# One more pair of up-projection strips by half-size products, and a new order of the steps around it

## The chip, the cores and the metric

The kernel runs on one core of one Trainium2 chip. The metric is device time of that core in microseconds (us): the median of three runs of the kernel before is 671.82 us (671.79 to 672.07). Times in traces count from the start of the profiled span. The engines are TensorE (PE; PEld is its weight load), VectorE (DVE), ScalarE (ACT), GpSimd (POOL) and SyncE (SP, which here only issues transfers).

## The reference, cut to what matters

One decoder layer: a mixing sub-layer, then a gated MLP with a causal convolution of width 3 between the up-projection and the activation. The change lies in the second sub-layer (512 tokens, model width 1024, hidden width 2816, all f32):

```python
h2 = rmsnorm(x, norm2_g[l]) * (1.0 + sc2) + sh2
u = causal_dwconv(h2 @ w_up[l], conv_w[l], conv_b[l])      # w_up: 1024 x 5632
a, v = jnp.split(u, 2, axis=-1)
x = x + gt2 * ((jax.nn.silu(a) * v) @ w_down[l])
```

## The kernel before, in words

**Strips.** The 5632 columns of `w_up` are 44 strips of 128. Strip st = 2f + s belongs to hidden block f (0 to 21); s = 0 is its half of `a`, s = 1 its half of `v`. Each strip ends up in one PSUM bank of 128 x 512 (`us[st]`). The normed input is kept as tiles `h2h` and `h2l`.

**High and low parts.** Every f32 operand is split into a high part, which ScalarE casts to the matmul's type, and a low part, the rest. A product is then three matmuls (`mm3`, lines 156 to 158): high by high, high by low, low by high; the last of the three is the first to read the weights' low part. `split` (lines 152 and 153) makes the low part by a VectorE subtraction. The adding form makes it without VectorE: ScalarE writes the negated rounded weights (line 263 or 1707), GpSimd issues a transfer that adds the weights to them in place (line 264 or 1708), and ScalarE casts the high part (line 265 or 1709).

**Two ways to multiply a strip pair.** A plain strip is 24 matmuls of 512 columns. The two strips of an even block f = 2j can instead be done together by seven half-size products (the Winograd scheme on 2 x 2 blocks: two strips, two halves of the 1024 inner rows, two halves of the 512 tokens). Each of the seven, P1 to P7, is 12 matmuls of 256 columns. It needs sums of the four weight quarters (`ns`, `nc`, `na`, `s4`: VectorE, in place on the loaded weights or in tile `e`), seven split forms of 512 columns (`n1` and `n5`, both in the single buffer of tile `w`, and `f2`, `f3`, `f4`, `f6`, `f7` in tiles `wq`), and four split sums of the input halves (`hS`, made once by the steps `t`). P1 adds up in `us[4j+1]`; `S` (ScalarE) copies that first result to the other strip's bank before P6 goes on in the same bank; P5 goes to a bank of its own, `ux`; `w` (ScalarE) copies that to SBUF; `V` and `W` (VectorE) add it back.

**Order.** Nothing reorders: each engine's queue runs in the order in which two strings of tokens are walked. `PRO` is the opening sequence (strips 0 to 7), `UNIT` is walked once for each j from 2 to 10 (strips 4j to 4j+3: a pair by half-size products, then two plain strips, cut into B0, B1 and C0, C1). A token with a prime prepares unit j + 1. M3 to M7 multiply plain strips, F and A split their weights (A by the adding form), q0 to q7 and p take a finished strip through the convolution (`up_post`, lines 1639 to 1655: an activation on ScalarE, a pair of VectorE steps, for s = 0 a silu on ScalarE, for s = 1 the gating product), x runs one piece of later work (sums and splits for the down-projection: `gP`, `gQ`, `st`, `s`), g and G advance the adaLN gate, m0 and m1 split the plain strips of a unit, h0 and h1 cast their high parts where these come later. In units j > 2 both low parts come by the adding form, in unit 2 only the second (line 1729).

**Loads.** SyncE loads the weights of one block (two strips) into one of three `raw` buffers (line 223); a load waits until the buffer's last readers are done.

Of the kernel before, what the change touches and what calls it, by code (L numbers as in the profile page):

```python
# [24 lines left out]
KT = D // P  # L25
# [15 lines left out]
NB = 2  # L41
NU = 10
AWAY = (0, 1, 2, 3, 4, 5)
CUT = {"B": 6, "C": 7}
ADD = (1, 1)
PLAIN = ""
PRO = ("t t x M1 M2 t t t t F3 M3 F4 t A5 q0 G M4 q1 q2 F6 q3 M5 G M6 A7 x q4 x q5 G x t x n1' ns' f2' nc' n5' q6 na' s4' m0' x x M7 m1' g x f6' f7' x x x x f4'")
UNIT = ("P1 S P5 w n1' ns' x f3 B0 P6 P2 B1 V x f2' nc' n5' h1 x p-1 f4' P7 x m0' P3 h0' W K p2 g na' p0 C0 P4 x x x C1 s4' p1 x m1' x f6' x x x f7'")
PREP = ('sq2 sq3 rq2 rq3', '', 'nq0', 'fq0', 'nq1', '', 'lq0', 'fq1', 'nq2', '', 'lq1', 'fq2', 'nq3', 'lq2', 'fq3',
        'lq3', 'sk0 rk0 sk1 rk1', 'nk0 fk0 sk2 rk2', 'nk1 fk1 sk3 rk3', 'lk0 nk2 fk2', 'lk1 nk3 fk3 sa0 ra0',  # L50
# [61 lines left out]
def hybrid_layer_kernel(ctx: ExitStack, tc: tile.TileContext, d: dict, out: bass.AP, dbg=None):  # L112
# [1552 lines left out]

    def h2_form(o, q):
        hS[q] = hi, lo = [G([4, 256], F32R, s="hS") for _ in range(2)]
        split(hi, lo, hB.pop(o))

    tw = [(h2_sum, (0, 0), (0, 1), (0, 0)), (h2_sum, (0, 1), (1, 1), (0, 1)), (h2_sum, (1, 1), (1, 1), (0, 0)),  # L1670
          (h2_form, (0, 0), 1), (h2_sum, (1, 0), (1, 0), (1, 1)), (h2_form, (1, 1), 2), (h2_form, (0, 1), 3),
# [7 lines left out]
    def half_form(src):  # L1679
        t = G([2, 4, P], F32R, s="wq")  # L1680
        split(t[:, 0], t[:, 1], src)
        return t[:, 0], t[:, 1]

    def pair_open(j):
        raw = take(f"up{2 * j}")
        quads[j] = [raw[:, s, 4 * h:4 * h + 4] for s in range(2) for h in range(2)]
        t = wp.tile([P, 2, KT, P], F32R, tag="aw", name=nm("w3"), bufs=1)
        forms7[j] = {n: (t[:, 0, h:h + 4], t[:, 1, h:h + 4]) for n, h in ((1, 0), (5, 4))}
        split(*forms7[j][1], quads[j][0])
# [35 lines left out]
    def std_make(j, s):  # L1725
        st = 4 * j + 2 + s
        if s == 0:
            raws[j] = take(f"up{2 * j + 1}")
        wts[st], high[st] = std_form(raws[j][:, s], ADD[s] and (s or j > NB))

    def seed(o, src):
        sc.copy(o, src)
# [3 lines left out]
        sc.copy(ws5[j], us["x", j][:, lo_half])  # L1736

    def banks(j):
        us[4 * j + 1] = PS("u")
        us["x", j] = PS("ux")  # L1740
        us[4 * j] = (held.pop if j == NU else held.get)(0)

    ws5 = {}

    def u_of(j, n, sl):
        return us[4 * j + n][:, sl]

    def do(j, tok):
        last = j == NU
# [8 lines left out]
    def do_(j, tok):  # L1758
        last = j == NU
        lo_, hi_ = lo_half, hi_half  # L1760
        w = forms7.get(j)
        u = partial(u_of, j)
        if tok == "P1":
            banks(j)
            sprod(u(1, lo_), w[1], h2_quarter(0, lo_), True)
            if last:
                pe.matmul(u(1, hi_), w[1][0][:, 0], h2_quarter(0, lo_)[0][0], start=False, stop=False,
                          skip_group_check=True)
        elif tok == "P5":
            sprod(us["x", j][:, lo_], w[5], h2_summed(1), True)  # L1770
        elif tok == "P6":
            sprod(u(1, lo_), w[6], h2_summed(2))
        elif tok == "P2":
            sprod(u(0, lo_), w[2], h2_quarter(1, lo_))
        elif tok == "P7":
            sprod(u(1, lo_), w[7], h2_summed(3))
        elif tok == "P3":
            sprod(u(0, hi_), w[3], h2_quarter(1, hi_))
        elif tok == "P4":
            sprod(u(1, lo_), w[4], h2_summed(4))  # L1780
        elif tok in ("B0", "B1", "C0", "C1"):
            up_mm(4 * j + (2 if tok[0] == "B" else 3), full, (range(0, CUT[tok[0]]), range(CUT[tok[0]], KT))[int(tok[1])])
        elif tok == "S":
            sc.copy(u(0, lo_), u(1, lo_))
        elif tok == "w":
            spare(j)
        elif tok == "V":
            ve.tensor_tensor(u(0, hi_), u(1, lo_), ws5[j], ALU.add)
        elif tok == "W":
            ve.tensor_tensor(u(1, hi_), u(1, lo_), ws5[j], ALU.add)  # L1790
        elif tok[0] == "p":
            up_post(4 * j + int(tok[1:]))
        elif tok == "x":
            step(1)
        elif tok in ("g", "G"):
            gate_step(2 if tok == "g" else 1)
        elif tok == "t":
            turn()
        elif tok[0] == "m":
            std_make(j, int(tok[1]))  # L1800
        elif tok[0] == "h":
            h = high.pop(4 * j + 2 + int(tok[1]))
            if h:
                h()
        elif tok == "K":
            park_late()
        elif tok == "n1":
            pair_open(j)
        elif tok == "ns":
            pair_sum(j)  # L1810
        elif tok == "nc":
            pair_less(j, 2, 0, 2)
        elif tok == "na":
            pair_less(j, 0, 4, 0)
        elif tok == "s4":
            pair_less(j, 1, 1, 0)
        elif tok == "n5":
            split(*w[5], quads[j][4])
        else:
            pair_form(j, int(tok[1]), {6: 0, 2: 1, 7: 2, 3: 1, 4: 3}[int(tok[1])])  # L1820
# [183 lines left out]
    for tok in PRO.split():  # L2004
        if tok[0] == "M":
            up_mm(int(tok[1]), full if tok[1] > "2" else hi_half)
            if tok == "M2":
                held[0] = us[0]
        elif tok[0] in "FA":
            piece(added=tok[0] == "A")  # L2010
            wts[int(tok[1])] = ahead.pop(0)
        elif tok[0] == "q":
            up_post(int(tok[1]))
        elif tok[0] in "txgG":
            do_(1, tok)
        else:
            do(NB - 1, tok)
# [111 lines left out]
```

## Time and profile before

| | us |
|---|---|
| median of three runs | 671.82 |
| profiled execution, its own time | 672.72 |
| its span | 670.9 |
| TensorE busy in the span | 663.2 |
| VectorE busy | 582.8 |
| ScalarE busy | 400.5 |
| last plain matmul run of the opening sequence starts (M7) | 367.0 |
| unit 2 starts (its P1) | 372.44 |
| unit 3 starts | 393.47 |
| down-projection starts | 562.25 |

A row of the timeline gives start, length, engine, line, operation, and written tile <- read tiles with their shapes; in brackets the idle time of that engine before it and what ended it. Consecutive rows of one engine overlap a little, so an engine's pace is read from starts.

### The profile page before, as it was taken

The page shows a single profiled execution, that of the slowest core. Times are in us where ns is not written, and L with a number is a line of the kernel's source. Part 1 is how long each engine was busy: PE and PEld are TensorE (multiplying, and loading weights), DVE is VectorE, ACT ScalarE, POOL GpSimd, SP SyncE. Part 2 cuts the span into 40 slices and gives each one's busy share as a digit, 9 for nine tenths or more (in the row PEclk, how much of TensorE's full clock was granted, in tenths as well). Part 3 has the DMA queues.
Part 4 walks back from the last instruction along what each step waited for, and adds up shares of the span by engine and source line. Part 5 has one row for each costly group of instructions (what it writes and reads, how often), then busy time and mean ns, then how long its engine had stood idle before and what let it go on. Part 6 is the DMA issues. An engine that isn't in the chain of part 4 may idle for free.

```text
span 670.9 us, 11080 instructions
## 1 busy us (share of the span) xinstructions
PE 663.2 (99%) x4072; PEld 567.9 (85%) x4072; DVE 582.8 (87%) x1173; ACT 400.5 (60%) x775; POOL 74.1 (11%) x100
## 2 busy tenths in 40 slices
PE   8999999999999999999999999999999999999997
PEld 4677898788898889888998989999899998888886
DVE  4688988999998997789988999888988888988787
ACT  5565446766677688334665776577765775553431
POOL 1006144200100000211100111010110110000000
PEclk9999999999999999999999999999999999999999
DMA  9999443398042132537436488877889759999932
GB/s 278 286 321 271 149 157 130 100 293 264 26 149 95 33 103 96 195 103 220 153 95 157 103 228 240 239 214 211 228 236 250 224 153 345 366 343 398 380 111 95
DMA packets 111880, 134.84 MB, mean 201 GB/s; under 512 B 7322, under 2 KB 84946, under 8 KB 111826
## 3 DMA queue, kind: packets, MB, share of 16 engines
q1 hardware_dynamic: 102961, 106.89, 50.2%
q0 software_dynamic: 4720, 16.26, 10.7%
q10 hardware_dynamic: 4144, 10.99, 4.3%
q8 instruction: 32, 0.52, 0.3%
q14 instruction: 23, 0.18, 0.1%
HBM read 107.11 MB, written 16.00 MB: 183 GB/s over the span
## 4 chain that ended last, share of the span: by engine, by line
PE 91%; SPq 3%; DMA 2%; DVE 2%; issue 1%; ACT 0%; ACTq 0%; DVEq 0%
PE u L157 11%; PE u L156 11%; PE u L158 11%; PE dn L157 5%; PE dn L156 5%; PE dn L158 5%; PE pT L156 3%; PE pT L158 3%; PE pT L157 3%; PE F L1063 3%; PE oT L1091 3%; PE oh L158 2%; PE oh L156 2%; PE oh L157 2%; PE lev L1192 2%; SPq L321 2%
## 5 line engine op out<-in xcount | busy, mean ns | idle before, releaser
L156 PE MATMUL u<-h2h,whi 128*128 128x512 f32 (+1 forms) x200 | 75.1, 375 | 0.0
L157 PE MATMUL u<-h2l,whi 128*128 128x512 f32 (+1 forms) x200 | 74.9, 374 | 0.0
L158 PE MATMUL u<-h2h,wlo 128*128 128x512 f32 (+1 forms) x200 | 74.5, 373 | 0.0
L158 PEld LDWEIGHTS u<-h2h,wlo 128*128 128x128 f32 x200 | 37.7, 189 | 6.8
L1031 ACT ACTIVATE pt<-pt,mx 128x128 f32<-128x128 f32 (+3 forms) x64 | 35.8, 562 | 12.1 <-DVE mx L1015 11.1
L156 PEld LDWEIGHTS u<-h2h,whi 128*128 128x128 f32 x200 | 37.9, 189 | 5.5
L157 PEld LDWEIGHTS u<-h2l,whi 128*128 128x128 f32 x200 | 37.9, 189 | 5.2
L156 PE MATMUL pT<-hT,whi 128*128 128x512 f32 x96 | 39.2, 409 | 0.0
L153 DVE TENSOR_TENSOR wlo<-raw,whi 128x1024 fp32r<-128x1024 f32 (+1 forms) x31 | 36.0, 1161 | 3.6 <-ACT whi L152 3.4
L1651 ACT ACTIVATE y<-y 128x512 f32<-128x512 f32 x22 | 13.9, 633 | 41.7 <-DVE y L1648 41.6
L158 PE MATMUL pT<-hT,wlo 128*128 128x512 f32 x96 | 37.7, 393 | 0.0
L157 PE MATMUL pT<-hT,whi 128*128 128x512 f32 x96 | 37.6, 392 | 0.0
L152 ACT CAST whi<-raw 128x1024 fp32r<-128x1024 f32 (+1 forms) x31 | 30.9, 998 | 10.4 <-PE kva L158 4.4
L1647 DVE SCALAR_TENSOR_TENSOR y<-u,cv,y 128x511 f32<-128x511 f32 x44 | 32.8, 745 | 5.0 <-ACT y L1646 5.0
L1070 ACT COPY pT<-F 128x512 f32<-128x512 f32 (+2 forms) x52 | 25.8, 502 | 15.4 <-PE F L1063 11.2
L1015 DVE CUSTOM_DVE_ANT_0 pt<-S,cmask 128x128 f32<-128x128 f32 (+3 forms) x64 | 29.7, 485 | 5.7 <-PE S L1010 5.6
L1648 DVE SCALAR_TENSOR_TENSOR y<-u,cv,y 128x510 f32<-128x510 f32 x44 | 32.9, 749 | 1.5
L397 POOL TENSOR_TENSOR hrs<-hrs,mhalf 128x4 f32<-128x4 f32 (+2 forms) x16 | 20.9, 1314 | 120.7 <-DVE hrs L396 120.6
L1646 ACT ACTIVATE y<-u,cv 128x512 f32<-128x512 f32 x44 | 33.8, 770 | 0.0
L1708 POOL DMA_DIRECT2D wlo<-raw x17 | 14.6, 859 | 166.2 <-ACT wlo L1707 74.6
L153 DVE TENSOR_TENSOR wq<-raw,wq 128x512 fp32r<-128x512 f32 x45 | 30.7, 685 | 0.5 <-ACT wq L152 0.5
L158 PE MATMUL u<-hS,wq 128*128 128x256 f32 x108 | 30.6, 284 | 0.0
(471 smaller groups left out, 2175.3 us busy)
## 6 DMA issues: line engine op xcount, KB each, us to landing
raw<-in_w_up SPq DMA_DIRECT2D x44, 512.0 KB, 5.7
aw<-in_w_ada SPq DMA_DIRECT2D x24, 512.0 KB, 3.8
raw<-in_w_down SPq DMA_DIRECT2D x10, 1024.0 KB, 5.4
wlo<-raw POOLq DMA_DIRECT2D x19, 512.0 KB, 5.2
ada<-in_w_ada SPq DMA_DIRECT2D x32, 256.0 KB, 5.9
raw<-in_w_in SPq DMA_DIRECT2D x7, 1024.0 KB, 6.0
rawd<-in_w_down SPq DMA_DIRECT2D x12, 512.0 KB, 10.5
pk<-st ACTq DMA_DIRECT2D x11, 512.0 KB, 6.5
```

Of the source, the lines that this page charges most:

```text
L152: sc.copy(hi, src)
L153: (eng or ve).tensor_tensor(lo, src, f32(hi), ALU.subtract)
L156: pe.matmul(o, ah, bh, start=start, stop=False, skip_group_check=True)
L157: pe.matmul(o, ah, bl, start=False, stop=False, skip_group_check=True)
L158: pe.matmul(o, al, bh, start=False, stop=stop, skip_group_check=True)
L397: gp.tensor_tensor(o, o, mhalf[:, 0:n], ALU.pow)
L1015: ve.tensor_tensor_reduce(pt[:, sl], ps[:, sl], cmask[:, 512 - W:512], -1.0, 1e30, ALU.add, ALU.min, mx[:, e:e + 1])
L1031: sc.activation(pt[:, sl], pt[:, sl], AF.Exp, bias=mx[:, e:e + 1], scale=-1.0, accum_out=su[:, h % 2, e:e + 1])
L1070: sc.copy(pT, ps[:, 0:n * P])
L1646: sc.activation(y, u, AF.Identity, bias=cv[:, 132 + c:133 + c], scale=cv[:, 88 + c:89 + c])
L1647: ve.scalar_tensor_tensor(y[:, 1:], u[:, :T - 1], cv[:, 44 + c:45 + c], y[:, 1:], ALU.mult, ALU.add)
L1648: ve.scalar_tensor_tensor(y[:, 2:], u[:, :T - 2], cv[:, c:c + 1], y[:, 2:], ALU.mult, ALU.add)
```

## The change

Block 3 (strips 6 and 7), which the opening sequence multiplied as two plain strips, becomes a tenth pair by half-size products, as "unit 1" with strips `base(1)` = 6 and 7. Its weights are taken as soon as token `no` is met. Strip 5 (M5) is multiplied in two pieces, Y0 and Y1, between those products. The opening string is written anew, with the preparation of unit 1 and of unit 2 in it. The low part of the fourth `hS` form comes by an adding transfer (`FADD`), and so does that of unit 2's first plain strip (`m0`).

```diff
--- before.py
+++ after.py
@@ -43,8 +43,9 @@
 AWAY = (0, 1, 2, 3, 4, 5)
 CUT = {"B": 6, "C": 7}
 ADD = (1, 1)
+FADD = (4,)
 PLAIN = ""
-PRO = ("t t x M1 M2 t t t t F3 M3 F4 t A5 q0 G M4 q1 q2 F6 q3 M5 G M6 A7 x q4 x q5 G x t x n1' ns' f2' nc' n5' q6 na' s4' m0' x x M7 m1' g x f6' f7' x x x x f4'")
+PRO = ("t t x M1 M2 t t t t F3 M3 F4 t A5 q0 no G ns nc M4 n1 q1 n5 t na f6 x f2 P1 S P5 w q2 s4 G x P6 P2 Y0 V x f7 q3 x P7 f3 f4 n1' G q4 P3 W m0' h0' Y1 q6 ns' nc' P4 n5' x f2' na' q5 f6' x s4' x m1' x g x f7' x x x f4'")
 UNIT = ("P1 S P5 w n1' ns' x f3 B0 P6 P2 B1 V x f2' nc' n5' h1 x p-1 f4' P7 x m0' P3 h0' W K p2 g na' p0 C0 P4 x x x C1 s4' p1 x m1' x f6' x x x f7'")
 PREP = ('sq2 sq3 rq2 rq3', '', 'nq0', 'fq0', 'nq1', '', 'lq0', 'fq1', 'nq2', '', 'lq1', 'fq2', 'nq3', 'lq2', 'fq3',
         'lq3', 'sk0 rk0 sk1 rk1', 'nk0 fk0 sk2 rk2', 'nk1 fk1 sk3 rk3', 'lk0 nk2 fk2', 'lk1 nk3 fk3 sa0 ra0',
@@ -1665,7 +1666,13 @@
 
     def h2_form(o, q):
         hS[q] = hi, lo = [G([4, 256], F32R, s="hS") for _ in range(2)]
-        split(hi, lo, hB.pop(o))
+        src = hB.pop(o)
+        if q in FADD:
+            sc.activation(lo, src, AF.Copy, scale=-1.0)
+            gp.dma_start(f32(lo), src, accum_op=ALU.add)
+            sc.copy(hi, src)
+        else:
+            split(hi, lo, src)
 
     tw = [(h2_sum, (0, 0), (0, 1), (0, 0)), (h2_sum, (0, 1), (1, 1), (0, 1)), (h2_sum, (1, 1), (1, 1), (0, 0)),
           (h2_form, (0, 0), 1), (h2_sum, (1, 0), (1, 0), (1, 1)), (h2_form, (1, 1), 2), (h2_form, (0, 1), 3),
@@ -1681,9 +1688,16 @@
         split(t[:, 0], t[:, 1], src)
         return t[:, 0], t[:, 1]
 
+    def base(j):
+        return 4 * j if j >= NB else 4 * NB - 2
+
+    def pair_take(j):
+        raw = take(f"up{base(j) // 2}")
+        quads[j] = [raw[:, s, 4 * h:4 * h + 4] for s in range(2) for h in range(2)]
+
     def pair_open(j):
-        raw = take(f"up{2 * j}")
-        quads[j] = [raw[:, s, 4 * h:4 * h + 4] for s in range(2) for h in range(2)]
+        if j not in quads:
+            pair_take(j)
         t = wp.tile([P, 2, KT, P], F32R, tag="aw", name=nm("w3"), bufs=1)
         forms7[j] = {n: (t[:, 0, h:h + 4], t[:, 1, h:h + 4]) for n, h in ((1, 0), (5, 4))}
         split(*forms7[j][1], quads[j][0])
@@ -1726,7 +1740,7 @@
         st = 4 * j + 2 + s
         if s == 0:
             raws[j] = take(f"up{2 * j + 1}")
-        wts[st], high[st] = std_form(raws[j][:, s], ADD[s] and (s or j > NB))
+        wts[st], high[st] = std_form(raws[j][:, s], ADD[s])
 
     def seed(o, src):
         sc.copy(o, src)
@@ -1736,14 +1750,14 @@
         sc.copy(ws5[j], us["x", j][:, lo_half])
 
     def banks(j):
-        us[4 * j + 1] = PS("u")
+        us[base(j) + 1] = PS("u")
         us["x", j] = PS("ux")
-        us[4 * j] = (held.pop if j == NU else held.get)(0)
+        us[base(j)] = (held.pop if j == NU else held.get)(0)
 
     ws5 = {}
 
     def u_of(j, n, sl):
-        return us[4 * j + n][:, sl]
+        return us[base(j) + n][:, sl]
 
     def do(j, tok):
         last = j == NU
@@ -1804,6 +1818,8 @@
                 h()
         elif tok == "K":
             park_late()
+        elif tok == "no":
+            pair_take(j)
         elif tok == "n1":
             pair_open(j)
         elif tok == "ns":
@@ -2006,6 +2022,8 @@
             up_mm(int(tok[1]), full if tok[1] > "2" else hi_half)
             if tok == "M2":
                 held[0] = us[0]
+        elif tok[0] == "Y":
+            up_mm(5, full, (range(0, 5), range(5, KT))[int(tok[1])])
         elif tok[0] in "FA":
             piece(added=tok[0] == "A")
             wts[int(tok[1])] = ahead.pop(0)
```

Two places of the engines' queues. First ScalarE, where the opening sequence ends and unit 2 is prepared (`y` are convolution results, `u` finished strips, `w<-raw` and `w<-e` the forms n1 and n5 of unit 2, `wlo` and `whi` the parts of its first plain strip, m0). In the kernel before:

```order
L152 CAST hS_4255<-hB_3726 128x1024
L152 CAST w_812_4263<-raw_4107 128x512
L152 CAST wq_4268<-raw_4107 128x512
L152 CAST w_812_4263<-e_4266 128x512
L1646 ACTIVATE y_4274<-u_4208,cv 128x512
L1651 ACTIVATE y_4274<-y_4274 128x512
L152 CAST whi_4284<-raw_4166 128x1024
L152 CAST gQ_4177<-y_4161 128x256
```

With the change:

```order
L153 CAST w_814_4299<-raw_4107 128x512
L1431 COPY gt_3318<-ps_4221 128x512
L1647 ACTIVATE y_4303<-u_4135,cv 128x512
L1652 ACTIVATE y_4303<-y_4303 128x512
L1721 ACTIVATE wlo_4325<-raw_4128 128x1024
L1723 CAST whi_4324<-raw_4128 128x1024
L1647 ACTIVATE y_4338<-u_3894,cv 128x512
L1652 ACTIVATE y_4338<-y_4338 128x512
L153 CAST w_814_4299<-e_4343 128x512
```

The cast of n5 stood two rows behind that of n1 and ahead of strip 6 and of m0. Now strip 4 (`u_4135`) with its silu, both steps of m0, and strip 6 (`u_3894`) with its silu stand between the two.

Second VectorE at the same place, from the low part of n1 of unit 2 to the low part of n5. In the kernel before:

```order
L153 TENSOR_TENSOR w_812_4263<-raw_4107,w_812_4263 128x512
L1693 TENSOR_TENSOR e_4266<-raw_4107 128x512
L153 TENSOR_TENSOR wq_4268<-raw_4107,wq_4268 128x512
L1698 TENSOR_TENSOR raw_4107<-raw_4107 128x512
L153 TENSOR_TENSOR w_812_4263<-e_4266,w_812_4263 128x512
```

With the change:

```order
L154 TENSOR_TENSOR w_814_4299<-raw_4107,w_814_4299 128x512
L1648 SCALAR_TENSOR_TENSOR y_4303<-u_4135,cv,y_4303 128x511
L1649 SCALAR_TENSOR_TENSOR y_4303<-u_4135,cv,y_4303 128x510
L1804 TENSOR_TENSOR u_4186<-u_4186,w5u_4213 128x256
L1648 SCALAR_TENSOR_TENSOR y_4338<-u_3894,cv,y_4338 128x511
L1649 SCALAR_TENSOR_TENSOR y_4338<-u_3894,cv,y_4338 128x510
L1707 TENSOR_TENSOR e_4343<-raw_4107 128x512
L1712 TENSOR_TENSOR raw_4107<-raw_4107 128x512
L154 TENSOR_TENSOR w_814_4299<-e_4343,w_814_4299 128x512
```

The sum `e`, from which n5 is made, followed n1 directly; now the convolution pairs of strips 4 and 6 and W of unit 1 come first.

## The prediction

> **What bounds the kernel now.** I read the page's busy line, then its chain of waits, then busy time by stage, and after that the timelines of single engines around the place of the change. The page's first part and the first line of its fourth:
>
> ```profile
> PE 663.2 (99%) x4072; PEld 567.9 (85%) x4072; DVE 582.8 (87%) x1173; ACT 400.5 (60%) x775; POOL 74.1 (11%) x100
> ...
> PE 91%; SPq 3%; DMA 2%; DVE 2%; issue 1%; ACT 0%; ACTq 0%; DVEq 0%
> ```
>
> TensorE is busy 99% of the span and 91% of the last chain. Busy time by stretch (start:end, length, then PE, PEld, DVE, ACT, POOL, clock, DMA): last 18.7 us of the setup, the opening sequence from M3 to M7, then units 2 and 3.
>
> ```profile
> 326.00:344.70 18.70, 18.70 (x160) 18.70 (x158) 18.43 (x34) 11.98 (x25) 0.55 (x1) 1.00 0.19 75
> 344.70:372.40 27.70, 27.70 (x124) 22.99 (x124) 21.85 (x33) 16.47 (x23) 1.83 (x2) 1.00 0.62 152
> 372.40:393.50 21.10, 21.10 (x134) 19.12 (x134) 19.23 (x35) 15.17 (x27) 3.37 (x5) 1.00 0.71 189
> 393.50:414.50 21.00, 21.00 (x134) 19.05 (x133) 18.92 (x35) 14.16 (x26) 2.28 (x3) 1.00 0.87 234
> ```
>
> TensorE has no gap in any of them. So what it no longer multiplies is won in full, and what it must wait for is lost in full, as long as nothing after it has slack to give back. The second engine is VectorE: in the opening sequence it has 27.70 - 21.85 = 5.85 us free, in a unit 2.1 us.
>
> **The products.** TensorE's timeline: M3 starts, M4 starts, M6 starts; unit 2's P1, its last product, a product of P5, and P6 (start, length; the starts give the pace, since ends overlap).
>
> ```profile
> 344.76 0.40 PE L156 MATMUL u<-h2h,w 128*128 128x512 f32 x1
> ...
> 350.23 0.39 PE L156 MATMUL u<-h2h,whi 128*128 128x512 f32 x1
> ...
> 361.56 0.39 PE L156 MATMUL u<-h2h,w 128*128 128x512 f32 x1
> ...
> 372.44 0.28 PE L156 MATMUL u<-h2h,w 128*128 128x256 f32 x1
> ...
> 373.75 0.28 PE L158 MATMUL u<-h2h,w 128*128 128x256 f32 x1
> ...
> 379.42 0.28 PE L156 MATMUL u<-hS,wq 128*128 128x256 f32 x1
> ```
>
> M6 and M7 are 48 products of 512 columns from 361.56 to 372.44: 10.88 us, 0.227 each. Twelve of 256 columns step from 372.44 to 373.75 in 11 intervals: 0.119 each, 1.43 for one P. Seven P are 84 x 0.1194 = 10.03. **Removed 10.88, added 10.03: 0.85 us won.** The weight loads, one for each product, run beside them at this pace already.
>
> **When the forms are ready.** Until M3 nothing differs. From there I lay out the new program with these starts. Unstalled, TensorE has M4 at 350.2, P1 at 350.23 + 5.44 = 355.65, P5 at 357.1, the gate's two products (0.45), P6 at 358.95, P2 at 360.4, Y0 (15 products) at 361.85, P7 at 365.25, P3 at 366.7, Y1 at 368.1, P4 at 370.15; then unit 2: P1 at 371.6, P5 at **373.0**, B0 at 374.45. ScalarE's rows give the pace of its queue: two casts of 512 columns, S, w, and the next cast; and, at M3, the adding form's two steps and the first up_post. The last of them is a silu, which waits for its own strip's two convolution steps on VectorE. VectorE's: two steps of 1024 columns, the two convolution steps, three of 512, two of 256.
>
> ```profile
> 418.24 0.62 ACT L152 CAST st<-s 128x512 fp32r<-128x512 f32 x1
> 418.76 0.62 ACT L152 CAST wq<-raw 128x512 fp32r<-128x512 f32 x1
> 419.29 0.36 ACT L1784 COPY u<-u 128x256 f32<-128x256 f32 x1
> 419.59 0.36 ACT L1736 COPY w5u<-ux 128x256 f32<-128x256 f32 x1
> 419.85 0.62 ACT L152 CAST w<-raw 128x512 fp32r<-128x512 f32 x1
> ...
> 344.96 1.06 ACT L263 ACTIVATE wlo<-raw 128x1024 fp32r<-128x1024 f32 x1
> 345.93 1.03 ACT L265 CAST whi<-raw 128x1024 fp32r<-128x1024 f32 x1
> 346.87 0.76 ACT L1646 ACTIVATE y<-u,cv 128x512 f32<-128x512 f32 x1
> ...
> 411.39 0.63 ACT L1651 ACTIVATE y<-y 128x512 f32<-128x512 f32 x1 [2.13 <-DVE y L1648]
> ```
>
> ```profile
> 343.58 1.22 DVE L153 TENSOR_TENSOR w<-raw,w 128x1024 fp32r<-128x1024 f32 x1
> 344.71 1.22 DVE L153 TENSOR_TENSOR wlo<-raw,whi 128x1024 fp32r<-128x1024 f32 x1
> ...
> 347.67 0.75 DVE L1647 SCALAR_TENSOR_TENSOR y<-u,cv,y 128x511 f32<-128x511 f32 x1 [0.60 <-ACT y L1646]
> 348.45 0.75 DVE L1648 SCALAR_TENSOR_TENSOR y<-u,cv,y 128x510 f32<-128x510 f32 x1
> ...
> 399.62 0.69 DVE L153 TENSOR_TENSOR wq<-raw,wq 128x512 fp32r<-128x512 f32 x1
> 400.22 0.68 DVE L153 TENSOR_TENSOR w<-raw,w 128x512 fp32r<-128x512 f32 x1
> 400.82 0.68 DVE L1693 TENSOR_TENSOR e<-raw 128x512 f32<-128x512 f32 x1
> ...
> 403.52 0.43 DVE L1788 TENSOR_TENSOR u<-u,w5u 128x256 f32<-128x256 f32 x1 [1.41 <-PE u L158]
> 403.86 0.42 DVE L153 TENSOR_TENSOR gP<-y,gP 128x256 fp32r<-128x256 f32 x1
> ```
>
> So a ScalarE cast of 512 takes 0.53 of its queue, S or w 0.30, a step over 1024 columns 0.95, an activation 0.67 and a silu 0.54 (their 0.76 and 0.63 less the tenth by which neighbours overlap); a VectorE step of 1024 takes 1.13, of 512 0.60, of 256 0.34, a convolution pair 0.78 + 0.74. Now down the queues.
>
> The pair's first forms are in time: n1 is cast at 351.1, the last of n5, f6, f2 leaves VectorE at 358.1, where P6 wants them at 358.95. Then **w** (ScalarE) must wait for P5's end at 358.65, and q2's activation stands behind it: 359.0 to 359.8. VectorE idles from 358.1 until then, and from 359.85 runs without a break through q2's pair (1.52), s4 (0.60), a sum (0.34), V (0.34), f7 (0.60), q3's pair (1.56), its gating product (0.60), a sum (0.34), f3, f4, n1' (1.80), q4's pair (1.52): 9.22, to 369.1. f7 (363.3 against P7 at 365.25) and f3 (366.45 against P3's first use of its low part at 366.9) are in time. q4's silu on ScalarE waits for that pair, and **m0'** is queued behind the silu, with two steps over 1024 columns; behind them q6's activation, behind that, on VectorE, q6's pair and the sum ns', and only then the form n5' of unit 2:
>
> silu 369.15, m0' low 369.7, m0' high 370.65, q6 371.6 to 372.4; VectorE q6's pair 372.4 to 373.9, ns' to 374.6; ScalarE n5' 374.65 to 375.27; VectorE its low part 375.3 to 376.0.
>
> P5 of unit 2 wants n5' at 373.0. How soon a product starts once its weights are written, these two rows tell (load starts, product starts):
>
> ```profile
> 662.16 0.19 PEld L156 LDWEIGHTS dn<-whi,A 128*128 128x128 f32 x1
> 662.38 0.39 PE L156 MATMUL dn<-whi,A 128*128 128x512 f32 x1
> ```
>
> 0.2 later: the high part lets P5 begin at 375.45, and its third product, on the low part, at 376.2 instead of 375.7. **First stall 2.45 + 0.5 = 2.95 us.** In the kernel before, n5' was cast at 369.2, while TensorE was in M7, 4.7 us ahead of P5; the second row is that kernel's S, for the next step:
>
> ```profile
> 369.21 0.62 ACT L152 CAST w<-e 128x512 fp32r<-128x512 f32 x1 [0.87 <-DVE e L1693]
> ...
> 378.25 0.36 ACT L1784 COPY u<-u 128x256 f32<-128x256 f32 x1
> ```
>
> B0 then runs from 377.4 and P6 of unit 2 is due at 377.4 + 18 x 0.227 = 381.5. It needs **S**, which saves P1's result first. ScalarE meanwhile: f2' 0.53, q5 0.67, then a wait for na' (VectorE n5' 0.60, a sum 0.34, f2' 0.60, na' 0.69: 377.55), f6' 0.53, gQ 0.30, m1' 0.95, st, gP 0.60, f7' 0.53, a wait of 0.2 for a sum, gQ 0.30, st 0.53, f4' 0.53: S from 382.0, done at 382.4. **Second stall 0.95 us.** Before, S started at 378.25 and P6 at 379.42.
>
> In unit 3 the same count gives S done at 402.9 and P6 due at 403.35: in time, and a unit's 2.1 us of VectorE's free time widens it. In every unit ScalarE also waits once for the plain weights of the next; they land up to 5.1 us after VectorE's last read (f3's low part) frees their buffer, which TensorE does not notice today:
>
> ```profile
> 422.45 0.68 DVE L153 TENSOR_TENSOR wq<-raw,wq 128x512 fp32r<-128x512 f32 x1
> ...
> 428.21 1.06 ACT L1707 ACTIVATE wlo<-raw 128x1024 fp32r<-128x1024 f32 x1 [2.89 <-DMA raw<-in_w_up]
> ```
>
> **Edits costed at nothing.** "no" only takes the load earlier; up3 has landed long before. hS form 4 by an adding transfer takes one VectorE step of 1024 away and puts one on ScalarE at 353, where n5 has just gone out and f6 still waits for VectorE. Two views of transfers (wlo as a whole; POOL's row):
>
> ```profile
> DMA to landing us min/median/max: 4.5/5.2/8.7
> ...
> 375.78 0.86 POOL L1708 DMA_DIRECT2D wlo<-raw x1 [15.57 <-ACT st L152]
> ```
>
> Issued at 354.5 it lands by 359 to 363; P4 wants it at 370.15. Without that cover it would cost up to 8.7. m0' by an adding transfer: POOL issues at 371.2, landing at 375.7 to 379.9, most nearly 376.4; B0's first use of the low part is at 374.9 unstalled, but 377.8 behind the first stall. So 0 at the median, 2.2 at the longest; were the first stall not there to hide it, 1.5 at the median. Its extra 0.95 of ScalarE is already in the first stall. The up6 load now waits for f4 (367.0) instead of the adding transfer of A7; its reader comes at 382.6. SP issues it past nothing else.
>
> **Sum.** -0.85 + 2.95 + 0.95 = +3.05. The profiled execution: span 670.9 becomes 673.95, its time 672.72 becomes 675.8; it lay 0.9 above the median. From the median 671.82: **674.9 us**. Bounds: if products start at once when a form is written, the waits shrink by 0.2 each and by what the queues' paces were rounded (some 25 steps at 0.02): 674.0; the other way 675.8.
>
> **Rivals.** 0.2% is 1.34 us, about what a measurement of this kernel tells from no change.
>
> *The forms keep up* (not slower): 671.82 - 0.85 = 671.0. For it: VectorE's 5.85 us free take the pair's extra work, seven half forms (4.20) and four sums (2.40), V and W (0.68), less the full steps of F6, m0 and hS (3 x 1.13): +3.9. Against it: that free time lies between 358 and 360 and after 369, in waits that the order itself makes. It decides if n5' is written by 372.8. Chance 0.10.
>
> *The adding transfer for m0' is late as well*: at its 8.7 another 2.2, 677.1. It decides from a landing of over 6.4 us. Chance 0.06.
>
> *A stalled TensorE restarts slowly.* The first eight small-type products after 1.59 us at rest, and the next eight:
>
> ```profile
> 1.59 3.60 PE L366 MATMUL warm<-wrm 128*128 128x512 bf16 x8 [1.59 <-DVE mhalf L368]
> ...
> 5.28 1.90 PE L383 MATMUL warm<-wrm 128*128 128x512 bf16 x8
> ```
>
> 3.60 against 1.90: 1.7 us more, so 676.6. Against it: no row inside the kernel shows it, as no wait there is long enough to. Chance 0.05. [...]
>
> *The lag never closes*: later loads come 5.5 us after their buffer is free instead of at most 5.1, S is late in each of the seven remaining units by some 0.6: 674.9 + 4.2 = 679.1. Against it is ScalarE's wait of 2.89 us in the row above, free of cost today. Chance 0.05.
>
> **Chances.** Forecast 0.72, the rivals 0.10, 0.06, 0.05, 0.05, and 0.02 for something that makes it clearly faster. Range 673.4 to 676.7: the forecast's own 674.0 to 675.8, widened down to where one stall is half as long and up to the slow restart. Faster by over 0.2% 0.02; within it 0.14 (the forms keep up, or the stalls are halved); slower 0.84.
>
> **What would show it.** TensorE's line in the changed trace must have a gap of 2 to 3 us in front of the ux products of unit 2, ended by the cast w<-e and then its VectorE step, and one of about 1 us in front of P6, ended by S (u<-u). VectorE must idle some 1.7 us before q2's pair and 3 us before q6's. The opening sequence to unit 2's P1 must be 0.85 shorter. After unit 3 every start must be later than before by the same amount. The forecast is wrong if unit 2's P5 follows P1 without a gap, if a gap stands in front of B0's low part, or if later units have gaps.

## The result, and the profile after

The changed kernel takes 676.19 us (median of four runs, 675.50 to 676.49) against 671.95 for the kernel before on the same chip (four runs, 671.79 to 672.85): ratio 1.0059, 95% interval 1.0042 to 1.0076. It is slower by about 4 us. The forecast was 674.9 with a range of 673.4 to 676.7. The profiled execution took 676.47, span 674.7, 3.8 more than the span before.

Busy time by stretch of the changed kernel (columns as in the prediction): the opening sequence, the end of it with the first product of unit 2, the rest of unit 2's first half, the rest of unit 2, most of unit 3.

```profile
344.70:372.00 27.30, 27.30 (x164) 24.34 (x163) 21.42 (x33) 18.39 (x28) 2.13 (x3) 1.00 0.61 149
372.00:376.00 4.00, 1.82 (x16) 1.62 (x14) 3.01 (x5) 2.34 (x5) 0.56 (x1) 1.00 0.84 166
376.00:381.00 5.00, 4.78 (x20) 4.00 (x20) 4.93 (x9) 3.90 (x9) 0.69 (x2) 0.66 0.02 5
381.00:397.50 16.50, 16.50 (x102) 14.83 (x101) 15.64 (x30) 10.53 (x19) 2.70 (x5) 1.00 0.83 226
397.50:414.50 17.00, 17.00 (x110) 15.47 (x109) 15.79 (x30) 12.89 (x23) 2.29 (x3) 1.00 0.84 217
```

All of the loss stands in 9 us, at the start of unit 2: TensorE lacks 2.2 us between 372 and 376, and between 376 and 381 it is busy at a granted clock of 0.66. TensorE's timeline there: the first and last product of P1, the first three of P5, then two of P5 and three of B0 at half pace, and two of B0 at the usual one.

```profile
371.99 0.28 PE L157 MATMUL u<-h2h,w 128*128 128x256 f32 x1
...
373.31 0.28 PE L159 MATMUL u<-h2h,w 128*128 128x256 f32 x1
375.76 0.39 PE L157 MATMUL ux<-hS,w 128*128 128x256 f32 x1 [2.17 <-ACT w L153]
375.99 0.28 PE L158 MATMUL ux<-hS,w 128*128 128x256 f32 x1
376.49 0.39 PE L159 MATMUL ux<-hS,w 128*128 128x256 f32 x1 [0.22 <-DVE w L154]
...
377.67 0.41 PE L157 MATMUL ux<-hS,w 128*128 128x256 f32 x1
377.89 0.41 PE L158 MATMUL ux<-hS,w 128*128 128x256 f32 x1
...
378.31 0.63 PE L157 MATMUL u<-h2h,whi 128*128 128x512 f32 x1
378.74 0.63 PE L158 MATMUL u<-h2l,whi 128*128 128x512 f32 x1
379.17 0.63 PE L159 MATMUL u<-h2h,wlo 128*128 128x512 f32 x1
...
380.95 0.39 PE L158 MATMUL u<-h2l,whi 128*128 128x512 f32 x1
381.18 0.40 PE L159 MATMUL u<-h2h,wlo 128*128 128x512 f32 x1
```

P5 waits for the high part of n5' and then for its low part: 375.76 - 373.31 - 0.12 = 2.33, and 376.49 - 375.99 - 0.12 = 0.38. Then products of 256 columns step 0.21 instead of 0.12 apart and products of 512 columns 0.43 instead of 0.23, from 377.07 to about 380.6. P5 to the end of B0 takes 7.70 us, of which 5.52 at the usual pace (1.43 + 18 x 0.227), 0.38 the second wait, and about 1.8 the half pace. P6 follows at 383.46 with no wait. ScalarE's queue shows what was late:

```profile
369.70 0.63 ACT L1652 ACTIVATE y<-y 128x512 f32<-128x512 f32 x1 [3.39 <-DVE y L1649]
370.24 1.04 ACT L1721 ACTIVATE wlo<-raw 128x1024 fp32r<-128x1024 f32 x1
371.19 1.03 ACT L1723 CAST whi<-raw 128x1024 fp32r<-128x1024 f32 x1
372.12 0.77 ACT L1647 ACTIVATE y<-u,cv 128x512 f32<-128x512 f32 x1
374.55 0.63 ACT L1652 ACTIVATE y<-y 128x512 f32<-128x512 f32 x1 [1.66 <-DVE y L1649]
375.09 0.62 ACT L153 CAST w<-e 128x512 fp32r<-128x512 f32 x1
...
382.27 0.36 ACT L1798 COPY u<-u 128x256 f32<-128x256 f32 x1
```

This is the chain that the prediction walked down: q4's silu, the two steps of m0', q6's activation, q6's pair on VectorE, and only then the cast of n5'. ScalarE is idle twice in it (3.39 and 1.66) with nothing but a silu at the head of its queue. S, the last row, would have held up P6 had B0 run at the usual pace.

Where the 3.8 us of span lie, by starts of the two traces:

| stretch | before | after | difference | forecast |
|---|---|---|---|---|
| span's start to M3 | 344.76 | 345.08 | +0.32 | 0 |
| M3 to unit 2's P1 | 27.68 | 26.91 | -0.77 | -0.85 |
| unit 2's P1 to unit 3's P1 | 21.03 | 25.52 | +4.49 | +3.90 |
| unit 3's P1 to the down-projection | 168.78 | 168.82 | +0.04 | 0 |
| the rest of the span | 108.65 | 108.37 | -0.28 | 0 |

### The profile page after: what moved, and what is told of

Read it like the earlier page. It is cut to its first block, busy times and chain, and to the rows that moved or that the text cites. A ratio compares the mean times of both kernels' runs of the same rounds, so it can differ in the third digit from the quotient of the medians.

```text
span 674.7 us, 11175 instructions
## 1 busy us (share of the span) xinstructions
PE 664.7 (99%) x4108; PEld 569.9 (84%) x4108; DVE 586.9 (87%) x1183; ACT 403.7 (60%) x783; POOL 75.0 (11%) x101
## 4 chain that ended last, share of the span: by engine, by line
PE 48%; DVE 6%; ACT 1%; DMA 1%; issue 1%; POOL 0%; ACTq 0%
PE u L158 10%; PE u L157 10%; PE u L159 10%; PE dn L158 5%; PE dn L159 5%; PE dn L157 5%; PE ux L159 1%; PE ux L158 1%; PE ux L157 1%; DMA gt<-in_w_ada 1%; DVE wol L154 1%; DVE hB L1552 1%; DVE tmp L1516 0%; DVE y L1649 0%; DVE y L1648 0%
## 5 line engine op out<-in xcount | busy, mean ns | idle before, releaser
L157 PE MATMUL u<-h2h,whi 128*128 128x512 f32 (+1 forms) x192 | 72.4, 377 | 0.0
L158 PE MATMUL u<-h2l,whi 128*128 128x512 f32 (+1 forms) x192 | 72.2, 376 | 0.0
L159 PE MATMUL u<-h2h,wlo 128*128 128x512 f32 (+1 forms) x192 | 71.6, 373 | 0.0
L154 DVE TENSOR_TENSOR wq<-raw,wq 128x512 fp32r<-128x512 f32 x50 | 34.1, 684 | 1.1 <-ACT wq L153 1.1
L153 ACT CAST wq<-raw 128x512 fp32r<-128x512 f32 x50 | 30.8, 617 | 5.8 <-DVE st L154 2.5
L159 PE MATMUL u<-hS,wq 128*128 128x256 f32 x120 | 34.0, 283 | 0.0
```

Of the source, the lines that this page charges most:

```text
L153: sc.copy(hi, src)
L154: (eng or ve).tensor_tensor(lo, src, f32(hi), ALU.subtract)
L157: pe.matmul(o, ah, bh, start=start, stop=False, skip_group_check=True)
L158: pe.matmul(o, ah, bl, start=False, stop=False, skip_group_check=True)
L159: pe.matmul(o, al, bh, start=False, stop=stop, skip_group_check=True)
```

## The experiments

Theory **Q**: what costs is the order of the queues; the forms of unit 2 come too late and TensorE waits, at worst with a slow restart behind the wait. Theory **W**: the work that the change adds (half forms, sums, adding transfers) costs time by itself.

### q4 behind m0'

```diff
-P7 f3 f4 n1' G q4 P3 W m0' h0' Y1
+P7 f3 f4 n1' G P3 W m0' h0' q4 Y1
```

A piece of the opening string; all else as in the changed kernel, so that m0' no longer stands behind q4's silu.

> The changed kernel with one token moved: q4 (strip 4's convolution) stands behind m0' and h0' instead of ahead of them, so that m0's two ScalarE steps fill the time in which ScalarE waited for q4's silu. Theory Q (the queues' order makes TensorE wait, and a long wait makes it restart slowly): the wait in front of unit 2's P5 shrinks from 2.7 us to about 1.5, too short for a slow restart, so the granted clock stays at 1.00; in its place the wait for S in front of P6, hidden by the slow clock before, shows with 0.8. Sum of waits 2.4 less 0.85 won: 672.0 + 1.5 = 673.5. Theory W (the added work of ScalarE and VectorE and the added transfers cost the time, in whatever order): no gain against the changed kernel, 675.5 to 676.5.

Measured 674.09 (nine runs; before 672.36, sixteen runs), ratio 1.0026, interval 1.0016 to 1.0035. TensorE's rows behind its waits, three in unit 2 and one in unit 3:

```profile
373.34 0.39 PE L157 MATMUL ux<-hS,w 128*128 128x256 f32 x1 [0.61 <-ACT w L153]
374.07 0.39 PE L159 MATMUL ux<-hS,w 128*128 128x256 f32 x1 [0.23 <-DVE w L154]
380.26 0.39 PE L157 MATMUL u<-hS,wq 128*128 128x256 f32 x1 [0.64 <-ACT u L1798]
...
398.24 0.50 PE L159 MATMUL u<-h2h,wlo 128*128 128x512 f32 x1 [0.23 <-DMA wlo<-raw]
```

By starts, as above, the gaps are 0.77, 0.39, 0.79 and 0.39. With the same work, moving one token took the first wait from 2.33 to 0.77 and 2 us out of the time. The pace stayed whole (products of B0 0.23 apart), and at once the wait for S stands where the prediction had it. The last row is a wait that nobody had forecast: unit 3's first product on a low part that an adding transfer makes. The time is 0.6 over the 673.5 expected. For Q.

### A wholly new order

```diff
-q0 no G ns nc M4 n1 q1 n5 t na f6 x f2 P1 S P5 w q2 s4 G x P6 P2 Y0 V x f7 q3 x P7 f3 f4 n1' G q4 P3 W m0' h0' Y1
+q0 no G ns x M4 nc q1 n1 t n5 f2 f4 q2 P1 na P5 s4 n1' q3 Y0 S x Y1 P2 G w f6 m0' g x x h0' f7 f2' f3 P6 m1' V P7
```

The tokens behind are in a new order too.

> The same products, sums, splits and transfers as the changed kernel; the opening string has another order (preparation of units 1 and 2 spread so that no form is behind a step that waits). Theory Q: no wait of TensorE from M3 to unit 4, granted clock 1.00, and what is left is the saving of the products: 672.0 - 0.85 = 671.1, faster than before by 0.13%. Theory W: the work is the same, so 674 or more.

A miss: 676.21 (median of five runs; a sixth took 1699.57 us and is left out), ratio 1.0055, 1.004 to 1.0069. The order removed both known waits and made a worse one. TensorE's row at P7, and ScalarE's and VectorE's row ahead of it:

```profile
370.31 0.41 PE L157 MATMUL u<-hS,wq 128*128 128x256 f32 x1 [3.09 <-DVE u L1802]
...
365.84 0.59 ACT L1431 COPY gt<-ps 128x512 f32<-128x512 f32 x1 [3.66 <-PE ps L1429]
...
367.93 1.90 DVE L154 TENSOR_TENSOR wq<-raw,wq 128x512 fp32r<-128x512 f32 x3 [4.19 <-ACT wq L153]
```

The gate's copy stood in ScalarE's queue ahead of three casts, but its product stood far back in TensorE's: the copy held ScalarE for 3.66 us, the casts came late to VectorE, V behind them, and TensorE waited 3.1 us for V and then had a mean clock of 0.54 from 370.3 to 374.0. Again an order, again a head of a queue that waits.

### Each adding transfer undone

The first kernel makes the low part of m0' by VectorE's subtraction as before; the second does so for the fourth `hS` form.

```diff
-        wts[st], high[st] = std_form(raws[j][:, s], ADD[s])
+        wts[st], high[st] = std_form(raws[j][:, s], ADD[s] and (s or j > NB))
```

> The changed kernel with unit 2's first plain low part (m0) by VectorE's subtraction as before, instead of by an adding transfer: ScalarE has one 1024-column step less (0.95) ahead of q6, VectorE one more of 1.13. Theory Q: the wait in front of P5 of unit 2 shrinks by about 0.5 us, from 2.7 to 2.2; whether the slow restart stays tells how long a wait it needs: 674.0 without it, 675.5 with it. Theory W, with the transfer as the cost: back to about 672.

```diff
-FADD = (4,)
+FADD = ()
```

> The changed kernel with the fourth hS form by VectorE's subtraction instead of by an adding transfer. Theory Q: that step lies where ScalarE and VectorE wait anyway, so the same waits and the same time as the changed kernel, 675.5 to 676.5. Theory W, with the transfer as a cost: 1 us or more faster.

One run each: 675.96 and 676.19 (changed kernel 676.19). Without m0's adding transfer the wait at P5 is 1.84 instead of 2.33, as ScalarE has one step of 1024 columns less ahead of q6, and the half pace follows as before (a clock of 0.53 from 377.0 to 380.5). Without that of the `hS` form nothing moves: TensorE is idle 2.2 and 0.2 us ahead of P5, as in the changed kernel. TensorE's row of the first:

```profile
375.01 0.38 PE L157 MATMUL ux<-hS,w 128*128 128x256 f32 x1 [1.69 <-ACT w L153]
```

So neither transfer is the loss. That B0 never waits for m0's low part in the changed kernel rules out the rival of the late adding transfer there.

### A second new order, with the gate's copy behind its product

```diff
-q0 no G ns nc M4 n1 q1 n5 t na f6 x f2 P1 S P5 w q2 s4 G x P6 P2 Y0 V x f7 q3 x P7 f3 f4 n1' G q4 P3 W m0' h0' Y1
+q0 no G G x M4 ns nc q1 n1 f2 f7 t n5 P1 q2 P5 na s4 x x n1' S ns' f6 Y0 w P2 nc' f3 f4 P6 V n5' G P7 q3 m0' h0' q4 P3 x na' W Y1
```

> A second new order of the opening string with all products, sums, splits and transfers of the changed kernel. In the first new order the gate's copy on ScalarE stood ahead of V's helpers while its two products stood late in TensorE's queue, so ScalarE waited 3.7 us, VectorE behind it, and P7 stood 3.25 us waiting for V; here the gate's products come ahead of M4 and no ScalarE step is queued behind a late product. Theory Q: no wait of TensorE over 0.4 us from M3 to unit 4, granted clock 1.00, time 672.2 - 0.85 = 671.4 (671.2 to 672.2). Theory W (the work itself costs the time): 674 or more, with waits again somewhere.

672.73 (eleven runs) against 672.63 (fifteen), ratio 1.0005, 0.9996 to 1.0014. All of the added work is in it and the loss is gone: W falls. Q's 671.4 (at most 672.2) was missed too. Nothing is won, because V and W come late for P7 and P4 of unit 1:

```profile
365.85 0.39 PE L157 MATMUL u<-hS,wq 128*128 128x256 f32 x1 [0.53 <-DVE u L1802]
...
371.43 0.36 PE L157 MATMUL u<-hS,wq 128*128 128x256 f32 x1 [0.38 <-DVE u L1804]
```

Their gaps of 0.68 and 0.54 eat the 0.85 of the products.

### Waits of a chosen length in the kernel before

To price a wait by itself, the kernel before was given one in unit 6, between P6 and P2: TensorE waits for a chain of small GpSimd steps (two, four or seven; two are shown).

```diff
+    dz = cst.tile([P, 1], F32, name="dz")
+    ve.memset(dz, 1.0)
...
+    def halt(bank):
+        pe.matmul(bank[:, 256:257], ident, dz, start=True, stop=True, skip_group_check=True)
+        for _ in range(2):
+            gp.tensor_tensor(dz, dz, mhalf[:, 0:1], ALU.pow)
+        pe.matmul(bank[:, 256:257], ident, dz, start=True, stop=True, skip_group_check=True)
...
             sprod(u(1, lo_), w[6], h2_summed(2))
+            if j == 6:
+                halt(us["x", j])
```

> The kernel before, with one artificial wait in TensorE's queue: in unit 6, between P6 and P2, TensorE stands until two small GpSimd steps are done that start when P6 is issued. Nothing else waits for them and nothing is left out. Expected wait 1.2 to 1.8 us. If a wait of TensorE passes in full to the end: the time is longer by just that wait. If later slack gives it back: less. Slow restart (pace of 512-column products 0.43 instead of 0.227): not after so short a wait.

> As the run with two small GpSimd steps, with four: a wait of 2.3 to 3.0 us, like the first wait of the changed kernel. Passed on in full, and if the slow restart needs only a wait of this length and nothing special of the changed kernel, about 3.4 us at half pace follow it, another 1.7 us: in all 4.0 to 4.7 us longer than before. If the slow restart had another cause: 2.3 to 3.0.

> As the run with two small GpSimd steps, with seven: a wait of 4 to 5 us. With the slow restart: 5.7 to 6.7 us longer than before, the extra 1.7 being the same as after the shorter wait, since the slow stretch has a length of its own and doesn't grow with the wait. Without: 4 to 5.

One run each: 671.87, 673.56, 676.99. The middle wait's row and the first product behind it, then the longest one's, the last product of P2 and the first of B1:

```profile
465.53 0.38 PE L1754 MATMUL ux<-dz,cb 128*128 128x1 f32 x2 [2.57 <-POOL dz L1753]
465.77 0.36 PE L156 MATMUL u<-h2h,wq 128*128 128x256 f32 x1
```

```profile
467.43 0.38 PE L1754 MATMUL ux<-dz,cb 128*128 128x1 f32 x2 [4.41 <-POOL dz L1753]
467.68 0.36 PE L156 MATMUL u<-h2h,wq 128*128 128x256 f32 x1
...
469.90 0.41 PE L158 MATMUL u<-h2h,wq 128*128 128x256 f32 x1
470.12 0.63 PE L156 MATMUL u<-h2h,whi 128*128 128x512 f32 x1
...
566.57 0.40 PE L156 MATMUL dn<-w,gP 128*128 128x512 f32 x1
```

From the end of P6 to P2 the three insert 1.85, 3.09 and 4.94 us. The second left the pace alone in its one execution, the third halved it for 3.4 us. But against the kernel before all three were 2.2 to 2.6 us too early, already at unit 2. That needed a base of its own.

### The tile alone, and the changed kernel with it

The three kernels with a wait have one more tile, `dz`. The next three have it too, and never read it: the kernel before, the changed kernel with its order mended (below), and the changed kernel as it is.

```diff
-f2 P1 S P5 w q2 s4 G x P6 P2 Y0 V x f7 q3 x P7 f3 f4 n1' G q4 P3 W m0' h0' Y1 q6 ns' nc' P4 n5' x f2' na' q5 f6' x s4'
+f2 P1 S P5 f4 w q2 s4 G x P6 P2 Y0 V x f7 q3 x P7 f3 n1' G P3 W m0' h0' q4 Y1 ns' nc' P4 n5' f2' q6 x na' x q5 f6' s4' x
```

> The kernel before with only the unused one-column tile dz and its memset behind mhalf, as the three kernels with an inserted wait have them, and no wait. Theory A (the tile shifts the places of all later buffers and the opening's transfers run faster for it): unit 2's ux products near 371.4 us instead of 373.87, the first DMA queue again near 340 GB/s in 4 to 50 us instead of 308, span near 668.5, time 669.4 to 670.3, ratio about 0.996. Theory B (the earlier start of the kernels with a wait has to do with the wait or with the chance of one profile): 671.8 to 672.8, ratio 1.000, opening at 308 GB/s. It is also the base that the inserted waits are measured from: with 1.85, 3.09 and 4.94 us of wait the spans were 670.1, 671.8 and 675.2, so under A a base of 668.3 means that the first two waits passed in full and the third cost 1.9 more.

> The changed kernel with the order of the steps mended (f4 ahead of w, f3 alone behind P7, q4 behind m0' and h0', q6 behind f2') and the tile dz. Theory Q (the order of the forms was the loss): PE waits 0 to 0.6 us in units 1 and 2, no slow pace, products 0.85 shorter: net -0.2 to -0.8 against the kernel with dz alone in this call, whatever that one gives; under A and Q 669 to 670, ratio 0.995. If V and W come late again as in the other new order, waits of 0.5 to 1.2 and a net of 0 to +0.4. Theory W (the added halves, products and transfers cost time of themselves): +1 us or more over the kernel with dz alone.

> The changed kernel as it is, with the tile dz. Theory Q: the waits at unit 2's P5 stand as before (2.2 to 2.5 and 0.4), so +2 us at least over the kernel with dz alone. On the slower pace behind the wait there are two theories. L (it follows a wait of that length at that place, whatever the moment): halved pace again, behind the wait 1.8 more, dn at +4.0 over the kernel with dz alone, S hidden. M (it depends on the moment at which the wait falls, as a wait of 2.57 us inserted in unit 6 left the pace alone and one of 1.69 in unit 2 did not): the pace may stay full, then P6 waits 0.8 to 0.95 for S and dn stands at +2.9 to +3.1.

Before 672.37 (fifteen runs). The kernel before with the tile: **669.98**, ratio 0.9965 (0.9951 to 0.9979). The mended order with it: **669.88**, 0.9962 (0.9949 to 0.9974). The changed kernel with it: 673.40, 1.0015 (1.0006 to 1.0024).

*The base.* With the tile alone the down-projection starts at 559.51. The three waits put it at 561.60, 563.14 and 566.57; less what each trace was late already at unit 2 (0.17, 0.47, 0.54 against 371.12) they cost 1.92, 3.16 and 6.52 for 1.85, 3.09 and 4.94 inserted. The two shorter ones were passed on in full, and the longest cost 1.6 on top, in the one of the three that had the half pace.

*The order.* The mended order against the tile alone: no difference (669.88 and 669.98), where the changed kernel loses 3.4. The wait at unit 2's P5 is gone. The net of -0.2 to -0.8 that Q expected was not reached: two waits eat its 0.85, S for P6 (gap 0.35), and the first adding transfer of unit 3 (gap 0.51):

```profile
376.15 0.39 PE L157 MATMUL u<-hS,wq 128*128 128x256 f32 x1 [0.19 <-ACT u L1800]
394.16 0.50 PE L159 MATMUL u<-h2h,wlo 128*128 128x512 f32 x1 [0.34 <-DMA wlo<-raw]
```

The second comes from unit 2's form f3 ending later on VectorE (380.02 instead of 378.63): the load of unit 3's plain weights is issued 1.4 us later than with the tile alone (380.05 instead of 378.65), and the transfer that adds them 1.3 later (385.28 instead of 384.00).

*The wait and the pace.* In the profiled run of the changed kernel with the tile the same two waits stand 2.7 us earlier in the run, and the pace behind them is whole. TensorE's rows, the last two in unit 3, and two stretches:

```profile
373.07 0.39 PE L157 MATMUL ux<-hS,w 128*128 128x256 f32 x1 [2.17 <-ACT w L153]
...
379.99 0.39 PE L157 MATMUL u<-hS,wq 128*128 128x256 f32 x1 [0.63 <-ACT u L1800]
...
397.33 0.40 PE L158 MATMUL u<-h2l,whi 128*128 128x512 f32 x1
397.84 0.50 PE L159 MATMUL u<-h2h,wlo 128*128 128x512 f32 x1
```

```profile
370.00:376.00 6.00, 3.61 (x24) 3.05 (x23) 5.66 (x10) 3.24 (x7) 0.00 (x0) 1.00 0.46 91
376.00:381.00 5.00, 4.37 (x23) 3.45 (x22) 4.97 (x11) 5.00 (x12) 1.95 (x3) 1.00 0.44 87
```

Now P6 does wait for S: gap 0.79. And unit 3 waits for its first adding transfer, as with q4 moved: gap 0.28 (the page puts 0.5 us of the idle time of the weight loads on that line down to the transfer wlo<-raw). The down-projection starts 3.91 later than with the tile alone, of which 0.38 were there at M3 already; the +2.9 to +3.1 of theory M had no term for unit 3. Of this kernel's ten timed runs six had a mean clock of 0.997, as the changed kernel's profiled run with the half pace had, and four of 1.000, and their times don't differ: 673.14 to 673.47 and one of 674.60 against 673.12 to 673.58. So one and the same wait had the half pace behind it in some executions of this case and not in others, by that clock. That rules out theory L and fits theory M, though what differs between the executions was not measured. And since the half pace gave S and the transfer their time, it cost next to nothing more here.

### A wider tile

```diff
-    dz = cst.tile([P, 1], F32, name="dz")
+    dz = cst.tile([P, 16], F32, name="dz")
```

> The kernel before with the unused tile dz and its memset, 64 bytes wide in each partition instead of 4. Places are handed out in steps of 32 bytes, so that the small dz moves every later buffer by 32 bytes and this one by 64: in the kernel before the buffers that the large transfers write begin at an odd multiple of 32 bytes (the first weight buffer at 151072), with the small dz at a multiple of 64, with this dz at an odd multiple of 32 again. Theory 64 (where the destination stands against 64 bytes sets the rate of the transfers): as before, 308 GB/s in the opening, ux products of unit 2 near 373.9 us, 671.8 to 672.8, ratio 1.000. Theory X (any extra tile and memset behind mhalf, or any shift, does it): 340 GB/s, ux products near 371.4, 669.6 to 670.4, ratio 0.9965.

672.20 (eleven runs), ratio 0.9997 (0.9988 to 1.0006): as before, so theory X is out. A tile and a memset by themselves don't bring the 2.4 us. What the compiled programs also differ in is where the later buffers stand: the first weight buffer begins at byte 151008 of its partition in the kernel before, at 151040 with the small tile and at 151072 with the wide one (the expectation gives this last figure for the kernel before). That the place is the cause is inferred from these three programs alone. The result is the one that theory 64 expected, but the one faster place, 151040, is a multiple of 64, of 128 and of 256, so the runs don't show what it is about a place that counts. Opening, 4 to 50 us: the transfers' mean rate and the first queue's share, of this kernel, and then of the one with the small tile (packets, bytes, packet time as a share of 16 engines).

```profile
DMA packets 21154, 14.50 MB, mean 315 GB/s; under 512 B 1637, under 2 KB 19197, under 8 KB 21150
...
q1 hardware_dynamic: 21099, 14.43, 109.2%
```

```profile
DMA packets 21831, 15.81 MB, mean 344 GB/s; under 512 B 1677, under 2 KB 19238, under 8 KB 21827
...
q1 hardware_dynamic: 21772, 15.74, 104.7%
```

Per MB the packets take 1.047 x 46 x 16 / 15.74 = 49.0 us of an engine with the first weight buffer at 151040, and 1.092 x 46 x 16 / 14.43 = 55.7 with it at 151072.

## Why the prediction was right, and where not

**Products, -0.85.** M3 to unit 2's P1 is 0.77 shorter. Right; that the rest are the starts of the first products behind a change of tile was not taken apart.

**First wait, 2.45 + 0.5.** Measured 2.33 + 0.38, ended by the two instructions named. The walk down the queues held to 0.25 us, once the 0.32 that the trace was late at M3 is taken off: q4's silu starts at 369.70 (forecast 369.15), m0' at 370.24 (369.7), the cast of n5' at 375.09 (374.65). VectorE is idle ahead of q2's pair and of q6's as forecast (1.7 and 3):

```profile
360.15 0.75 DVE L1648 SCALAR_TENSOR_TENSOR y<-u,cv,y 128x511 f32<-128x511 f32 x1 [1.62 <-ACT y L1647]
...
372.92 0.75 DVE L1648 SCALAR_TENSOR_TENSOR y<-u,cv,y 128x511 f32<-128x511 f32 x1 [2.98 <-ACT y L1647]
```

Too long was the 0.2 from written weights to a product: the cast ends at 375.71 and P5 starts at 375.76. That it is this chain, two experiments show: moving q4 took 1.56 us of the wait away, and the mended order, with q6 later too, all of it.

**Second wait, 0.95 for S.** Not there in the profile of the changed kernel; 0.79 in the profiles of the two kernels whose pace stayed whole behind P5 (q4 behind m0', and the changed kernel with the tile). The cause was right; another delay covered it.

**Sum, 3.90 of waits in unit 2.** Where the pace is whole, unit 2 of the changed kernel with the tile takes 394.23 - 369.30 = 24.93 against 21.03: +3.90. That this meets the forecast to the hundredth is luck: the three gaps are 2.33 + 0.38 + 0.79 = 3.50, which is 0.40 less than forecast, and most of the rest are slower starts: behind each wait the first product steps some 0.22 instead of 0.12 (373.07 to 373.29), for which the forecast had no term. It had none for unit 3's adding transfer either: from unit 3's P1 to the down-projection this kernel takes 563.42 - 394.23 = 169.19 against 168.78. From M3 to the down-projection that makes 221.03, which is 3.54 more than the 217.49 before, where the forecast has 3.05. In the profile of the changed kernel, with the half pace, unit 2 is +4.49, unit 3 shows no wait, and M3 to the down-projection takes 221.25 (+3.76).

**Slow restart of TensorE, chance 0.05.** This is the step that failed, with little effect on the sum. "Against it: no row inside the kernel shows it, as no wait there is long enough to" was an absence of evidence, and it was priced as one. The half pace came in the profile and, by the mean clock, in three of the four runs; the fourth, at 1.000, took 676.49, no less than they. Its gross price was right (1.7 forecast, 1.8 measured), but the rival added it to the full sum (676.6), while in the kernel it runs over the time in which S and unit 3's transfer were late: 221.25 - 221.03 = 0.2 net in these two traces, and the ten runs of the changed kernel with the tile show no difference at all. What sets off the half pace, and when, was not shown. By the steps of the products it lasted about 3.4 us in each of three traces: 377.1 to 380.55 in the changed kernel, 376.9 to 380.3 without m0's adding transfer, 468.0 to 471.4 behind the longest inserted wait, so no longer behind 4.94 us of wait than behind 2.33 + 0.38. Nor did it always begin with the first product behind the wait: at once in the first new order, 0.3 us later behind the longest inserted wait, 1.3 in the changed kernel and 1.8 without m0's adding transfer. Waits of 2.33 + 0.38, and of 1.84 + 0.38, had it behind them in these traces; the inserted one of 2.57 in a single piece (3.09 from P6's end to P2) did not in its one execution.

**The base.** The forecast stood on a median of 671.82 from three runs. The fifteen or sixteen runs of the same kernel in later comparisons have medians of 672.31 to 672.63 and reach from 671.72 to 673.55: the three lay at the low end. By these, about 0.5 of the 1.3 between 674.9 and 676.2 is this, and 0.7 the stretch from M3 to the down-projection (+3.76 for +3.05: of this 0.08 in the products and 0.59 in unit 2). The 0.32 before M3 is of the size by which executions differ: M3 starts between 344.22 and 345.08 in the kernels without the tile. The -0.28 at the end is not: the rest of the span is 108.37 to 108.44 in every kernel with the change and 108.50 to 108.70 in every one without; its cause is open. So the forecast met its range, but by its width: 676.19 lies above the forecast's own 674.0 to 675.8, in the part that was added for the slow restart.

**Edits costed at nothing.** The adding transfer for the `hS` form cost nothing (same waits without it), and that of m0' nothing behind the first wait. The rival that it is late was false in unit 2; in the mended order, where the first wait is gone, an adding transfer is late in unit 3, by 0.5. That is the wait for the load behind f3 "which TensorE does not notice today": it does notice where the forms come later and no half pace covers it (0.28, 0.39 and 0.51 in the three kernels that show it).

**The forms keep up, chance 0.10.** False for this order, but "for it" was right: VectorE's free time does take the work, as the second new order and the mended one show. What it was to give, 0.85, no order tried here gave: the best ended at -0.10 us, within what a measurement can tell. Whether an order without any wait exists was not settled.

**Lag that never closes.** False as priced: unit 3 to the down-projection is 168.82 against 168.78. With the pace whole, the lag costs 0.41 once, in unit 3, and nothing after it; the prediction named gaps in later units as a sign against it, and there was this one.

## What to carry to other kernels

Here TensorE was busy without a gap, and cutting 0.77 us of its work paid nothing, as the preparation of what follows was moved behind something that waits: walk down each queue and look for an instruction at the head that must wait for another engine (here a silu, idle 3.39 us, and a gate's copy, 3.66), and count what stands behind it. Price a wait on TensorE at its length (here 1.92 and 3.16 us for 1.85 and 3.09 inserted). Behind waits of 1.84 + 0.38 us and longer the half pace came on top in some executions of this case, at up to 1.8 us: look at what the slower pace covers before adding the two. Take the base from many runs (here the median of three was some 0.5 low), and give any variant that adds a tile a control with the tile alone (here 2.4 us faster).

## What the runs showed of the hardware that was not expected

With the small tile, whose program has all later buffers 32 bytes further on in each partition (the first weight buffer at 151040 instead of 151008), the kernel before took 669.98 us instead of 672.37: 2.4 less, more than any order gave. With the wide tile, 64 bytes further on (151072), it took 672.20. The opening transfers ran at 344 GB/s with the small tile (333 to 343 in the five other kernels that have it), at 308 in the kernel before and at 315 with the wide one. TensorE gains in the opening: in 4 to 50 us it is busy 45.12 us instead of 43.94, and the first products that write `pT`, at 96.83 in the kernel before, start at 94.31 in the run with the short wait, which has the small tile too.

```profile
4.00:50.00 46.00, 43.94 (x262) 29.10 (x261) 32.74 (x103) 27.75 (x57) 3.68 (x6) 1.00 1.10 308
```

```profile
4.00:50.00 46.00, 45.12 (x269) 30.48 (x268) 34.97 (x108) 27.93 (x57) 3.69 (x6) 1.00 1.05 344
```

The first row is the kernel before, the second that with the small tile. Unit 2's ux products start 2.75 us earlier (371.12 against 373.87) and the down-projection 2.74 (559.51 against 562.25): from unit 2 to there nothing more is won, though the buffers of those loads stand 32 bytes further on too. Which of the buffers matters was not tried, since all moved together. The kernel before with the tile and the mended order with it are the fastest kernels of this study, equal within their spread.
